# Moving the second copies of the mLSTM query tiles by DMA inside SBUF

## The chip, the cores and the metric

One core of a Trainium2 chip runs the whole program; inputs and outputs lie in HBM. The metric is device time in microseconds (us) of one execution, taken as the median over several runs. The engines are TensorE (PE; its weight loads are shown as PEld), VectorE (DVE), ScalarE (ACT), GpSimd (POOL) and SyncE (SP); each works through its own queue of instructions in order and waits on semaphores for the others.

## The reference

A two-layer model on 512 tokens of width 1024 in float32. Layer one is a dilated window attention, layer two an mLSTM; each is followed by a SwiGLU feed-forward block of inner width 2816, and a final RMS norm ends it. The part that matters here is the mLSTM mixer, cut to its core:

```python
qk = silu(causal_depthwise_conv(xn @ w_qk, conv_w, conv_b))
q  = heads(qk[..., :512], 64)                 # 8 heads of 64
k  = heads(qk[..., 512:], 64) * 64 ** -0.5
...
w_intra = exp(dmat - m_t[..., None])          # decay from the gates
sm  = w_intra * einsum('bhtd,bhsd->bhts', q, k)
num = einsum('bhts,bhsv->bhtv', sm, v) + ...  # state carried from earlier chunks
den = sum(sm, axis=-1) + ...
h   = num / maximum(abs(den), exp(-m_t))[..., None]
h   = h * rsqrt(mean(h * h, axis=-1, keepdims=True) + eps)
out = (h * head_gain * sigmoid(o_pre)) @ w_out
```

The kernel does not carry a state from chunk to chunk: it forms the 512 x 512 scores of each head below the diagonal and weighs them with the decay.

## The kernel before

**Tiling.** Activations lie transposed, features on the 128 partitions and the 512 tokens along the free dimension. Each float32 operand of a large matmul is split into a high part in the format float32r and the rest in the same format, and a product is the sum of three matmuls (`SPLITS`): high by high, low by high, high by low. Weights come from HBM in chunks of 512 KB on SP's queue, ACT makes the high part (line 208) and DVE the low part (line 209), three chunks deep.

**The mLSTM stage.** `project_qk` and `convolve` make the query tiles `qk[0..3]` and the key tiles `qk[4..7]` (128 partitions hold two heads of 64): DVE multiplies by the norm's factor (line 1139) and adds four shifted products (lines 1146 and 1148), ACT applies SiLU (line 1150). `project_v` makes the values; ACT writes them to `vaug` (line 1161). The order of projections is: pairs of query and key tiles, then values, then the output gates (`mo`), then `mwo`, the output projection.

**The stacks.** `stack(p)` prepares the operands of the score matmuls of heads 2p and 2p+1. A head has only 64 features, so 128 partitions hold two things at once: `ks` has the high part of the keys on the head's own half of the partitions and the low part on the other half. `qs` has the high part of the queries on both halves, and `ql` the low part on both halves. One matmul of `ks` with `qs` then gives high by high plus low by high, and one with `ql` adds the rest. Own and other half are the slices `own` and `oth`. Before the change ACT writes both halves of `qs` (lines 1291 and 1292); DVE writes the own half of `ql` (line 1294), and POOL copies it to the other half (line 1295). Each of `ks`, `qs`, `ql` has two buffers per position in the pair, so that the third call of `stack` reuses the tiles of the first.

**Per head.** `decay` makes a matmul into the single PSUM buffer with tag `t` (name m0nb for head 0), DVE adds the causal mask to it (m0d, line 1306) and ACT takes exponentials from both (m0e, lines 1311 and 1314). `scores` multiplies (PE, lines 1324 and 1325, into two buffers with tag `s`) and DVE weighs (line 1326). `numerators` multiplies by the values (line 1336), ACT sums squares (line 1350), DVE takes three Newton steps for the root (lines 188 to 193) and scales (m0yt, line 1357). `outputs` transposes on PE (m0yT, line 305, again the buffer `t`), and ACT copies (line 1366).

**Order.** Work that lies beside the projections is put off to counted ticks, one for each weight chunk; `STACK_AT` and `HEAD_AT` give the ticks:

```python
STACK_AT = (9, 11, 15, 17)
HEAD_AT = ((9, 10, 12, 14), (10, 11, 13, 15), (12, 13, 15, 17), ...
```

Within these limits the framework's scheduler, at build time, fixes the order of the instructions of each engine from estimated durations, and places the semaphores. An edit to one instruction can therefore change the order of others.

Of the kernel before, what the change touches and what calls it, by code (L numbers as in the profile page):

```python
# [11 lines left out]
F32 = mybir.dt.float32  # L12
F32R = mybir.dt.float32r
I32 = mybir.dt.int32
AF = mybir.ActivationFunctionType
# [55 lines left out]
def tile_hybrid_dilated_attn_mlstm(  # L71
# [4 lines left out]
    nc = tc.nc  # L76
# [3 lines left out]
    def pool(stack, name, **kw):  # L80
        return stack.enter_context(tc.tile_pool(name=name, bufs=1, **kw))
# [1039 lines left out]
    with ExitStack() as mctx:  # L1121
# [160 lines left out]
        def stack(p):  # L1282

            for i in range(2):
                own, oth = slice(i * 64, i * 64 + 64), slice(64 - i * 64, 128 - i * 64)
                q, k = qk[p][own], qk[4 + p][own]
                ks = mp.tile([P, SEQ], F32R, tag="ks%d" % i, name="ks%d_%d" % (p, i), bufs=2)
                qs = mp.tile([P, SEQ], F32R, tag="qs%d" % i, name="qs%d_%d" % (p, i), bufs=2)
                nc.scalar.activation(ks[own], k, AF.Copy)  # L1289
                nc.vector.tensor_tensor(ks[oth], k, ks[own].bitcast(F32), op=ALU.subtract)  # L1290
                nc.scalar.activation(qs[own], q, AF.Copy)
                nc.scalar.activation(qs[oth], q, AF.Copy)  # L1292
                ql = mp.tile([P, SEQ], F32R, tag="ql%d" % i, name="ql%d_%d" % (p, i), bufs=2)
                nc.vector.tensor_tensor(ql[own], q, qs[own].bitcast(F32), op=ALU.subtract)
                nc.gpsimd.tensor_copy(ql[oth], ql[own].bitcast(F32))
                stacks[2 * p + i] = (ks, qs, ql)

        y = [None] * H
# [72 lines left out]
        for p, t in enumerate(STACK_AT):  # L1371
            at_tick(t, lambda p=p: stack(p))
# [161 lines left out]
```

## Time and profile before

| | us |
|---|---|
| median of 3 runs | 1432.88 (1432.66 to 1432.92) |
| the profiled execution | 1432.49 |
| its span, first to last instruction | 1430.7 |
| PE busy | 1418.7 (99%) |
| DVE busy | 955.7 (67%) |
| ACT busy | 604.6 (42%) |
| POOL busy | 61.1 (4%) |

The span is what the profile shows; the profiled execution took 1.8 us more than its span. Durations in the text are of that one execution. In the timelines the first number is the start in us from the span's beginning, the second the time in us that a row takes together; idle time ahead of a row and what ended it stand in brackets. Matmuls are pipelined, so that the rows of PE overlap and the distance between two starts is what one costs. In part 5 of a page and in the waits a wait for several semaphores is put down to the one that came last by the profile.

### The profile page before, as it was taken

How to read it: one execution, taken by the hardware profiler on the slowest of the kernel's cores; microseconds unless marked ns; L12 is line 12 of the kernel's file. 1: busy time of each engine (PE TensorE's matmuls, PEld its weight loads, DVE VectorE, ACT ScalarE, POOL GpSimd, SP SyncE). 2: the span in 40 equal slices, each digit the busy share in tenths (PEclk: the TensorE clock that was granted, in tenths of full speed). 3: DMA queues.
4: the chain of work that ended last, by engine and by line, in shares of the span. 5: the costliest groups of instructions: out<-in, count | busy, mean ns of one | idle time of the engine just before them, and what ended most of it. 6: DMA issues, size and time to landing. Idle time of an engine off the chain costs nothing. (4 is left out here: it accounts for less than half of the span.)

```text
span 1430.7 us, 20253 instructions
## 1 busy us (share of the span) xinstructions
PE 1418.7 (99%) x8018; PEld 1244.3 (87%) x8018; DVE 955.7 (67%) x1671; ACT 604.6 (42%) x1025; POOL 61.1 (4%) x101
## 2 busy tenths in 40 slices
PE   9999999999999999999999999999999999999997
PEld 7888888888888888999998888888888899998886
DVE  7857556556567397787782358897758777888233
ACT  5333224224215253444462233696534354455123
POOL 1001001001001000000000010110000000001001
PEclk9999999999999999999999999999999999999999
DMA  6326225234334434323232332312133332236331
GB/s 198 97 89 198 75 89 181 92 98 128 136 101 109 145 111 133 99 79 118 89 97 96 96 98 75 104 59 61 51 115 95 123 118 85 93 118 182 113 112 65
DMA packets 132088, 154.46 MB, mean 108 GB/s; under 512 B 6485, under 2 KB 120469, under 8 KB 131993
## 3 DMA queue, kind: packets, MB, share of 16 engines
q1 hardware_dynamic: 125616, 131.55, 29.4%
q0 software_dynamic: 4720, 20.49, 4.8%
q8 instruction: 63, 1.03, 0.3%
q10 hardware_dynamic: 1656, 1.12, 0.2%
q14 instruction: 33, 0.26, 0.1%
HBM read 141.09 MB, written 12.06 MB: 107 GB/s over the span
## 5 line engine op out<-in xcount | busy, mean ns | idle before, releaser
L1463 PE MATMUL fin<-fw_l,f1hh 128*128 128x512 f32 (+1 forms) x198 | 72.5, 366 | 0.0
L1463 PE MATMUL fin<-fw_h,f1hh 128*128 128x512 f32 (+1 forms) x198 | 72.4, 366 | 0.0
L1463 PE MATMUL fin<-fw_h,f1hl 128*128 128x512 f32 (+1 forms) x198 | 72.4, 365 | 0.0
L209 DVE TENSOR_TENSOR fo_k_l<-fo_k_w,fo_k_h 128x1024 fp32r<-128x1024 f32 (+1 forms) x24 | 27.2, 1134 | 62.0 <-ACT fo_k_h L208 62.0
L239 PE MATMUL fo<-f0hh,fo_k_h 128*128 128x512 f32 x176 | 68.5, 389 | 0.0
L239 PE MATMUL fo<-f0hl,fo_k_h 128*128 128x512 f32 x176 | 68.5, 389 | 0.0
L239 PE MATMUL fo<-f0hh,fo_k_l 128*128 128x512 f32 x176 | 68.5, 389 | 0.0
L209 DVE TENSOR_TENSOR fw_l<-fw_w,fw_h 128x1024 fp32r<-128x1024 f32 x22 | 27.0, 1232 | 59.9 <-ACT fw_h L208 59.9
L208 ACT ACTIVATE fo_k_h<-fo_k_w 128x1024 fp32r<-128x1024 f32 (+1 forms) x24 | 23.7, 989 | 74.7 <-PE fo L239 74.7
L208 ACT ACTIVATE fw_h<-fw_w 128x1024 fp32r<-128x1024 f32 x22 | 23.3, 1060 | 67.5 <-PE fin L1463 67.0
L1463 PEld LDWEIGHTS fin<-fw_l,f1hh 128*128 128x128 f32 x198 | 37.4, 189 | 6.2 <-DVE fw_l L209 0.2
L1463 PEld LDWEIGHTS fin<-fw_h,f1hh 128*128 128x128 f32 x198 | 37.4, 189 | 6.1
L1463 PEld LDWEIGHTS fin<-fw_h,f1hl 128*128 128x128 f32 x198 | 37.3, 188 | 6.0
L239 PEld LDWEIGHTS fo<-f0hh,fo_k_l 128*128 128x128 f32 x176 | 33.0, 188 | 6.9
L239 PEld LDWEIGHTS fo<-f0hl,fo_k_h 128*128 128x128 f32 x176 | 33.0, 188 | 6.9
L239 PEld LDWEIGHTS fo<-f0hh,fo_k_h 128*128 128x128 f32 x176 | 33.0, 188 | 6.7
L239 PE MATMUL f0j<-n_h,f0j_h 128*128 128x512 f32 x96 | 37.5, 390 | 0.0
L239 PE MATMUL f1j<-n_h,f1j_h 128*128 128x512 f32 x96 | 37.5, 390 | 0.0
L239 PE MATMUL f1j<-n_h,f1j_l 128*128 128x512 f32 x96 | 37.4, 389 | 0.0
L239 PE MATMUL f0j<-n_h,f0j_l 128*128 128x512 f32 x96 | 37.4, 389 | 0.0
L239 PE MATMUL f0j<-n_l,f0j_h 128*128 128x512 f32 x96 | 37.3, 389 | 0.0
L239 PE MATMUL f1j<-n_l,f1j_h 128*128 128x512 f32 x96 | 37.3, 389 | 0.0
(2101 smaller groups left out, 4863.2 us busy)
## 6 DMA issues: line engine op xcount, KB each, us to landing
f0j_w<-in_ffn_w_in_dram SPq DMA_DIRECT2D x28, 512.0 KB, 4.4
f1j_w<-in_ffn_w_in_dram SPq DMA_DIRECT2D x28, 512.0 KB, 3.6
fw_w<-in_ffn_w_out_dram SPq DMA_DIRECT2D x22, 512.0 KB, 3.9
fo_k_w<-in_ffn_w_out_dram SPq DMA_DIRECT2D x20, 512.0 KB, 3.5
awo_k_w<-in_attn_w_out_dram SPq DMA_DIRECT2D x8, 512.0 KB, 6.8
mv_k_w<-in_mlstm_w_in_dram SPq DMA_DIRECT2D x8, 512.0 KB, 3.7
mqk_k_w<-in_mlstm_w_in_dram SPq DMA_DIRECT2D x8, 512.0 KB, 3.8
mo_k_w<-in_mlstm_w_in_dram SPq DMA_DIRECT2D x8, 512.0 KB, 3.7
```

Of the source, the lines that this page charges most:

```text
L208: nc.scalar.activation(hi[:, :n], raw[:, :n], AF.Copy)
L209: nc.vector.tensor_tensor(lo[:, :n], raw[:, :n], hi[:, :n].bitcast(F32), op=ALU.subtract)
L239: nc.tensor.matmul(acc, whl[a][:, k, m * P:(m + 1) * P], pairs[b][kk], start=(kk == 0 and (a, b) == SPLITS[0]), stop=(kk == nk - 1 and (a, ...
L1463: nc.tensor.matmul(acc[i][:, cs], a[a_][kk][:, tb * P:(tb + 1) * P], whl[b_][:, k, cs], start=(kk == 0 and (a_, b_) == SPLITS[0]), stop=(k ...
```

## The change

In `stack`, for each of the eight heads, two copies to the other half of the partitions change their maker. The other half of `qs` was written by ACT from the float32 tile `q`; it is now a DMA from the own half of `qs`. The other half of `ql` was copied by POOL; it is now a DMA from the own half of `ql`. Both DMAs are issued from POOL's queue.

```diff
@@ -1289,10 +1289,10 @@
                 nc.scalar.activation(ks[own], k, AF.Copy)
                 nc.vector.tensor_tensor(ks[oth], k, ks[own].bitcast(F32), op=ALU.subtract)
                 nc.scalar.activation(qs[own], q, AF.Copy)
-                nc.scalar.activation(qs[oth], q, AF.Copy)
+                nc.gpsimd.dma_start(qs[oth], qs[own])
                 ql = mp.tile([P, SEQ], F32R, tag="ql%d" % i, name="ql%d_%d" % (p, i), bufs=2)
                 nc.vector.tensor_tensor(ql[own], q, qs[own].bitcast(F32), op=ALU.subtract)
-                nc.gpsimd.tensor_copy(ql[oth], ql[own].bitcast(F32))
+                nc.gpsimd.dma_start(ql[oth], ql[own])
                 stacks[2 * p + i] = (ks, qs, ql)
```

The instructions of SP stand in the same order before and after. On PE, DVE and ACT the first place where the order differs is in the mLSTM stage, and the number of matmuls, of DVE instructions and of ACT table loads is the same; ACT has eight instructions fewer, POOL eight casts fewer and sixteen DMA issues more.

## The prediction

> **What bounds the kernel now.** I read the page first, then the table of windows, TensorE's waits, and the timelines of PE, DVE and ACT around the edited lines.
>
> ```profile
> span 1430.7 us, 20253 instructions
> ...
> PE 1418.7 (99%) x8018; PEld 1244.3 (87%) x8018; DVE 955.7 (67%) x1671; ACT 604.6 (42%) x1025; POOL 61.1 (4%) x101
> ```
>
> TensorE is busy for 1418.7 of 1430.7 us. An engine beside it costs time only where PE waits for it. The edited copies run between 898 and 962 us; the table of windows gives span, then busy time and instructions of PE, PEld, DVE, ACT and POOL:
>
> ```profile
> 895.00:915.00 20.00, 20.00 (x142) 18.29 (x141) 19.70 (x30) 14.69 (x21) 2.80 (x3) 1.00 0.36 106
> 915.00:935.00 20.00, 19.62 (x104) 16.44 (x103) 15.98 (x29) 13.96 (x31) 1.67 (x1) 1.00 0.29 83
> 935.00:955.00 20.00, 20.00 (x126) 17.68 (x125) 19.32 (x56) 19.80 (x51) 2.20 (x2) 1.00 0.16 49
> 955.00:975.00 20.00, 18.33 (x124) 16.74 (x123) 15.39 (x47) 14.69 (x34) 1.75 (x2) 1.00 0.21 58
> ```
>
> PE is full, but here its two helpers nearly are too: DVE has 19.70 of 20 us in the first window, ACT 19.80 in the third. PE's waits from 880 to 1060 us:
>
> ```profile
> PE m1yT L305 <- ACT vaug L1161: 1.7, 1, 1.7
> PE m1nb L1304 <- ACT m0e L1314: 0.4, 1, 0.4
> ```
>
> So 2.1 us is all that a lighter ACT or DVE can give back in this stage, and a later instruction on DVE or ACT is paid in full if PE waits for it at these two places, or at a new one.
>
> **The change part by part.** *Removed.* The tile views of qs and ql give the old copies:
>
> ```profile
> L1292 ACT ACTIVATE qs<-mqk x8: 627/630/630, 899.0 to 958.4; 64x512 fp32r<-64x512 f32 x8
> ```
> ```profile
> L1295 POOL CAST ql<-ql x8: 612/1100/1667, 901.5 to 960.5; 64x512 fp32r<-64x512 f32 x8
> ```
>
> ACT loses 8 x 0.63 = 5.0 us, POOL 8 casts of 0.6 to 1.7 us. Neither bounds the kernel, so by themselves they are worth 0, or up to 2.1 us if they end PE's two waits (a rival below).
>
> *Added.* Sixteen copies of 64 x 512 x 4 bytes = 128 KB go onto POOL's queue. Nearest rows (issues with KB and median us to landing, then POOL's timeline):
>
> ```profile
> hD<-hB POOLq DMA_DIRECT2D x8, 256.0 KB, 5.8
> ...
> a3pT<-a3pD POOLq DMA_DIRECT2D x2, 960.0 KB, 9.3
> ...
> out_dram<-fo SPq DMA_DIRECT2D x4, 256.0 KB, 2.1
> ```
> ```profile
> 121.01 2.22 POOL L684 DMA_DIRECT2D a0pD<-a0pB  x4 [107.12 <-DVE a0pB L681]
> ...
> 1276.16 2.63 POOL L1422 DMA_DIRECT2D hD<-hB  x4 [238.09 <-DVE hB L1419]
> ```
>
> No transfer inside SBUF is in this trace, and none with fp32r tiles at both ends. I bound the landing by 2.1 and 9.3 us and take 5, near the 5.8 us of the POOL queue's own 256 KB transfers. An issue takes 2.22/4 = 0.56 us; POOL has the room. What hides the landing is the distance from ql's subtraction on DVE to the first score matmul that reads it. It is shortest for the first pair of heads: ql is complete at 900.67 + 1.40 = 902.07, and PE reads it at 915.94.
>
> ```profile
> 900.67 1.40 DVE L1294 TENSOR_TENSOR ql<-mqk,qs 64x512 fp32r<-64x512 f32 x2
> ```
> ```profile
> 915.94 0.40 PE L1325 MATMUL m0s<-ql,ks 128*128 128x512 f32 x1
> ```
> ```profile
> L1324 PE MATMUL m2s<-qs,ks x4: 220/346/390, 938.2 to 940.5; 128*128 128x512 f32 x1, 128*128 128x384 f32 x1, 128*128 128x256 f32 x1, 128*128 128x128 f32 x1
> ...
> L1324 PE MATMUL m6s<-qs,ks x4: 284/350/393, 991.2 to 994.4; 128*128 128x512 f32 x1, 128*128 128x384 f32 x1, 128*128 128x256 f32 x1, 128*128 128x128 f32 x1
> ```
>
> That is 13.9 us of cover; even 9.3 us plus three queued issues (1.7) is inside it. For later pairs the cover is longer (the last old cast starts at 960.5, its pair's first score at 991.2), and POOL's in-order queue (the third pair's second qs stands behind its first ql, which waits for DVE) has the same cover. Behind the sixteen copies POOL has nothing but a memset until the residual transfers at 1276 us. ACT's write of the third pair's qs reuses the first pair's buffer and must now also wait for that copy, due by 902.07 + 9.3 = 911 us; the buffer is read until the scores from 915.94 on anyway. SP's order of weight loads is unchanged. So the transfers cost 0; each microsecond of landing over 13.9 would cost one.
>
> *Moved.* The instruction order is fixed when the program is built, and the new order differs on PE, DVE and ACT. Three moves matter.
>
> (A) On DVE the second pair's two subtractions (L1294) go ahead of the convolution of the key tiles, instead of after the mask addition of head 0 (m0d); on ACT the last ks copy (L1289) goes ahead of head 0's exponentials, instead of after them. The rows of before, DVE, ACT and PE:
>
> ```profile
> 896.37 0.48 DVE L1146 TENSOR_SCALAR conv<-pre,cols 128x512 f32<-128x512 f32 x1
> ...
> 902.83 0.67 DVE L1146 TENSOR_SCALAR conv<-pre,cols 128x512 f32<-128x512 f32 x1
> ...
> 913.11 0.67 DVE L1294 TENSOR_TENSOR ql<-mqk,qs 64x512 fp32r<-64x512 f32 x1
> ...
> 914.52 1.00 DVE L1294 TENSOR_TENSOR ql<-mqk,qs 64x512 fp32r<-64x512 f32 x1
> ```
> ```profile
> 911.79 0.72 ACT L1150 ACTIVATE mqk<-conv,cols 128x512 f32<-128x512 f32 x1 [0.79 <-DVE conv L1148]
> ...
> 913.19 1.28 ACT L1311 ACT_TABLE_LOAD   x1
> ...
> 916.63 0.38 ACT L1314 ACTIVATE m0e<-m0nb,bcol 128x128 f32<-128x128 f32 x1
> ...
> 918.78 0.63 ACT L1289 ACTIVATE ks<-mqk 64x512 fp32r<-64x512 f32 x1
> ```
> ```profile
> 917.07 0.50 PE L1304 MATMUL m1nb<-mneg,sel 128*128 128x512 f32 x1 [0.38 <-ACT m0e L1314]
> ```
>
> Two subtractions back to back take 1.40; the convolution step that ran beside a POOL cast took 0.67 where its clean form takes 0.48, so 0.19 goes with the cast: the key tile's convolution ends 1.40 - 0.19 = 1.2 us later. ACT was waiting for exactly that (0.79 of idle time, ended by conv), so its SiLU, table load and exponentials move by 1.2, and by 0.63 more for the ks copy put in front. The last read of head 0's PSUM tile (916.63) and with it the next matmul into that single buffer, m1nb, come 1.2 + 0.63 = 1.8 us later; with the semaphores of the new neighbours I take 1.9. PE already waited there, so all of it is lost: **+1.9** (1.2 if the ks copy found idle time, 2.1 at most).
>
> (B) At m1yT PE waits 1.67 us:
>
> ```profile
> 941.55 0.15 DVE L1354 TENSOR_TENSOR m0rr<-m0rr,m0rq_y 128x4 f32<-128x4 f32 x1
> ...
> 942.79 0.68 DVE L1139 TENSOR_TENSOR pre<-mqk,n2rbc 128x512 f32<-128x512 f32 x1
> ...
> 958.50 0.69 DVE L1290 TENSOR_TENSOR ks<-mqk,ks 64x512 fp32r<-64x512 f32 x1
> 959.22 0.46 DVE L1354 TENSOR_TENSOR m1rr<-m1rr,m1rq_y 128x4 f32<-128x4 f32 x1
> ...
> 960.43 1.13 DVE L1357 TENSOR_SCALAR m1yt<-m1num,m1rr 128x128 f32<-128x128 f32 x4
> 961.47 1.22 DVE L209 TENSOR_TENSOR mo_k_l<-mo_k_w,mo_k_h 128x1024 fp32r<-128x1024 f32 x1
> ```
> ```profile
> 958.86 0.28 PE L271 MATMUL mv<-mv_k_h,n_h 128*128 128x256 f32 x1
> 958.98 0.28 PE L271 MATMUL mv<-mv_k_l,n_h 128*128 128x256 f32 x1
> 960.93 0.30 PE L305 MATMUL m1yT<-cst,m1yt 128*128 128x128 f32 x1 [1.67 <-ACT vaug L1161]
> ```
>
> The list names vaug, but m1yT reads m1yt, whose first piece starts at 960.43. In the new DVE order the 1.22 us split of mo_k_l moves ahead of m1yt, a ks subtraction of 0.69 moves behind it, and the stretch that casts put on rows like 959.22 (0.46 where its kind takes 0.15) goes; together about 0. So m1yt is late by what PE is late. But the new PE order puts five more value matmuls (0.12 us from start to start) ahead of m1yT: 0.6 of the wait is filled. Against that I keep 0.1 for DVE: **-0.5** (bounds -1.7, the whole wait, and 0).
>
> (C) Later, the second halves of the scores of heads 5, 6 and 7 and the transposes m3yT and m6yT change places with projection matmuls, and on DVE their predecessors stand between Newton steps and gate multiplications (128x512, as L1139 above 0.68 us). None of these places waits in before. Each of five (m3yT, m6s, m7s, m6yT, first use of yo_l) may get a wait between 0 and 0.7; I take 0.3, near the one short wait of the list (0.4): **+1.5** (0 to 3.5).
>
> Sum 1.9 - 0.5 + 1.5 = **+2.9 us**. The profiled execution took 1432.49 us, its span 1430.7 plus 1.8 around it; the median of the runs is 1432.88. On the median: **1435.8 us**. This case's own range adds the ends: 1.2 - 1.7 + 0 = -0.5, and 2.1 + 0 + 3.5 = +5.6, so 1432.4 to 1438.5.
>
> **The rivals.** *Not slower: ACT's returned time decides.* If it is really vaug on ACT that ends m1yT's wait, as the list says, four qs copies (2.5 us) leave ACT ahead of it after 933 us, the 1.67 us go, and with no loss at m1nb the 0.38 too: 1432.88 - 2.1 = 1430.8. It decides if ACT and not the DVE convolution is last ahead of m0e. Against it stands the 0.79 us idle ended by conv. Chance 0.07.
>
> *Absorbed.* If DVE has room so that m1yt does not move with PE, the 1.67 us wait swallows most of the 1.9, and (C) is zero: +0.2, 1433.1. For it: DVE loses the cast stretches. Against: it is 19.32 of 20 us busy there. Chance 0.15.
>
> *The transfers arrive late.* If the landing in this stage is over 13.9 us, PE stands at m0s: at 18 us it is +4.1 on top of +2.9, 1439.9. Chance 0.10, because issues in the trace beside DVE's work keep 0.56 us, and the longest landing is 9.3. [...] The trace shows the contention for casts (0.67 against 0.48 above) and not for the issue rows.
>
> **How the numbers follow.** Forecast case 0.68, rivals 0.07, 0.15, 0.10. A measurement of this kernel can tell about 0.2%, 2.9 us, from no change. The forecast sits on that bound. Its lower end needs m1yT's whole wait to go, which DVE at 19.32 of 20 us makes unlikely, while new waits at more places than five only add; so of its 0.68 I put 0.44 above the bound and 0.24 within. With the late transfers slower has 0.54; same is 0.24 + 0.15 = 0.39; faster 0.07. The range from 1432.4 to 1438.5 leaves out the gain, most of the late transfers and little else.
>
> **What would show it.** Right: PE's waits name m1nb with about 2.3 us, m1yT with about 1.1, and some of 0.2 to 0.6 at m3yT, m6s, m7s, m6yT; DVE shows L1294 four times before 907 us; the DMA part shows the copies landing in 2 to 9 us; conv rows beside them stay at 0.48. Wrong: m1nb's wait stays at 0.4, or PE waits at L1324 or L1325 for a DMA.

## The result and the profile after

The changed kernel takes 1437.18 us (median, 1436.16 to 1437.64), the kernel before 1432.93 (1432.44 to 1433.49): slower by 4.25 us, ratio 1.0029, 95% interval 1.0018 to 1.0039. The profiled execution took 1436.49 us, 4.0 more than that of before. First the busy times on the page, then the windows of the prediction:

```profile
span 1434.7 us, 20276 instructions
...
PE 1420.0 (99%) x8018; PEld 1245.1 (87%) x8018; DVE 954.8 (67%) x1671; ACT 599.2 (42%) x1017; POOL 60.7 (4%) x109
```
```profile
895.00:915.00 20.00, 20.00 (x137) 18.14 (x136) 19.68 (x31) 10.53 (x15) 4.10 (x8) 1.00 0.66 159
915.00:935.00 20.00, 17.84 (x99) 15.12 (x98) 13.93 (x24) 13.20 (x31) 0.00 (x0) 1.00 0.27 80
935.00:955.00 20.00, 20.00 (x119) 17.50 (x118) 19.15 (x58) 19.36 (x49) 2.55 (x5) 1.00 0.34 86
955.00:975.00 20.00, 18.89 (x132) 17.50 (x131) 15.15 (x46) 14.70 (x35) 1.53 (x3) 1.00 0.30 73
```

ACT has its 4 us back in the first window (10.53 for 14.69). PE has lost 1.8 us in the second (17.84 for 19.62) and found 0.6 in the fourth (18.89 for 18.33). TensorE's waits between 880 and 1060 us name the places, and the timelines of PE and DVE show them:

```profile
PE m1nb L1304 <- ACT m0e L1314: 2.2, 1, 2.2
PE m1yT L305 <- DVE m1yt L1357: 1.1, 1, 1.1
PE m6yT L305 <- DVE m6yt L1357: 0.3, 1, 0.3
```
```profile
919.85 0.50 PE L1304 MATMUL m1nb<-mneg,sel 128*128 128x512 f32 x1 [2.16 <-ACT m0e L1314]
...
963.39 0.30 PE L305 MATMUL m1yT<-cst,m1yt 128*128 128x128 f32 x1 [1.11 <-DVE m1yt L1357]
```
```profile
901.68 1.40 DVE L1294 TENSOR_TENSOR ql<-mqk,qs 64x512 fp32r<-64x512 f32 x2
...
904.85 0.67 DVE L1294 TENSOR_TENSOR ql<-mqk,qs 64x512 fp32r<-64x512 f32 x1
905.45 0.47 DVE L1146 TENSOR_SCALAR conv<-pre,cols 128x512 f32<-128x512 f32 x1
905.95 0.69 DVE L1294 TENSOR_TENSOR ql<-mqk,qs 64x512 fp32r<-64x512 f32 x1
```

The transfers themselves are fast: DMA issues with KB and median us to landing, and the tile view of qs with the issue's own ns:

```profile
qs<-qs POOLq DMA_DIRECT2D x8, 128.0 KB, 4.0
...
ql<-ql POOLq DMA_DIRECT2D x8, 128.0 KB, 2.9
```
```profile
L1292 POOL DMA_DIRECT2D qs<-qs x8: 509/512/529, 900.2 to 958.1; - x8
```

But the stage explains only a part of the 4.0. I followed the start of one and the same instruction through both traces. The first pair of rows is a0g0q on PE, before and after; the second the last group of PE in the chain that ended last; the third is POOL's drains, from the view of the program's last line (shortest/median/longest ns of three; the longest is the one that counts, below "the long drain"):

```profile
8.34 0.50 PE L449 MATMUL a0g0q<-xa_h,first_h 128*128 128x512 f32 x1 [0.51 <-ACT first_h L439]
```
```profile
9.25 0.49 PE L449 MATMUL a0g0q<-xa_h,first_h 128*128 128x512 f32 x1 [0.51 <-ACT first_h L439]
```
```profile
1302.54 120.80 PE fin L1463 x594
```
```profile
1305.25 120.80 PE fin L1463 x594
```
```profile
L1530 POOLq DRAIN  x3: 46/98/5512, 1424.4 to 1430.4; - x3
```
```profile
L1530 POOLq DRAIN  x3: 46/98/6817, 1427.1 to 1434.4; - x3
```

So PE is 0.9 late at the first product, 1.0 late in front of the edited stage, 2.7 late behind it: the stage costs 1.7. At the end POOL's long drain, which nothing in the edit names, takes 6.82 us instead of 5.51, and in both profiles the program ends 0.8 us after it: 1.3 more. The 1.0 at the start has to be scatter or a cost; in ten further profiles below, with and without transfers, the same lag against the one profile of before lies anywhere between -0.1 and 1.1 us, so it is scatter of the start. It goes with the granted clock, whose first record of 1.00 begins at 4.69 us in the trace of before and at 7.22 us in that of the changed kernel: the first matmuls of the program (line 107, 128x512) start 0.43 us apart ahead of it and 0.23 behind it. Over all twelve profiles this record begins between 4.39 and 7.69 us, and a later one always goes with a later a0g0q (8.03 to 9.35 us).

That gave three theories to test. **Order**: the stage loses because the scheduler moved the second pair's subtractions and the ks copy (term A). **Drain**: POOL's long drain takes 0.082 us more for each DMA issued from POOL's queue in the whole program (57 before, 73 after). **Transfers**: each copy by DMA costs something where it runs. A fourth, the **clock**, came from the first round.

### The profile page after: what moved, and what is told of

Same layout as the page of the kernel before. It is cut to its first block, busy times and chain, and to the rows that moved or that the text cites. A ratio compares the mean times of both kernels' runs of the same rounds, so it can differ in the third digit from the quotient of the medians.

```text
span 1434.7 us, 20276 instructions
## 1 busy us (share of the span) xinstructions
PE 1420.0 (99%) x8018; PEld 1245.1 (87%) x8018; DVE 954.8 (67%) x1671; ACT 599.2 (42%) x1017; POOL 60.7 (4%) x109
```

## The experiments

All ran with timed rounds beside the kernel before. "Lag" is how much later the same matmul of the last feed-forward stage starts than in the profile of before, less the same difference ahead of the edited stage. The diffs are cut to the lines that matter, with long lines broken.

| kernel | POOL's DMAs | m1nb's wait | lag over the stage | long drain | median less before's |
|---|---|---|---|---|---|
| before | 57 | 0.4 | 0 | 5.51 | 0 |
| changed | 73 | 2.2 | +1.7 | 6.82 | +4.25 |
| changed, second round (after_again) | 73 | 2.2 | +1.6 | 6.81 | +3.9 |
| qs_alone | 65 | 3.3 | +5.5 | 6.16 | +7.2 |
| ql_alone | 65 | 0.3 | -0.6 | 6.16 | +0.4 |
| sub_late | 73 | 0.6 | +0.1 | 6.82 | +1.2 |
| on_sp | 57 | 2.2 | +3.2 | 5.51 | +2.9 |
| order_alone | 57 | 1.4 | +1.7 | 5.51 | +1.8 |
| small64 | 121 | 0.4 | 0.0 | 10.74 | +5.2 |
| filled9 | 73 | none | +1.6 | 6.82 | +2.9 |
| ks_late | 73 | 1.5 | +1.0 | 6.82 | +2.35 |
| best | 47 | none | -1.0 | 4.69 | -1.9 |

**One kind of copy at a time.** qs_alone is the kernel before with only the line of qs changed, ql_alone with only that of ql.

```diff
-                nc.scalar.activation(qs[oth], q, AF.Copy)
+                nc.gpsimd.dma_start(qs[oth], qs[own])      # qs_alone
...
-                nc.gpsimd.tensor_copy(ql[oth], ql[own].bitcast(F32))
+                nc.gpsimd.dma_start(ql[oth], ql[own])      # ql_alone
```

> Only the second copies of qs go by DMA (8 transfers); those of ql stay casts on POOL. The instructions of PE, DVE and ACT stand in the order of the changed kernel. Three theories for the 4.25 us between the medians. Order theory: the stage loses because the second pair's subtractions stand ahead of the key convolution, so m1nb waits again about 2.5 us (2.2 in the changed kernel, a little more because the casts beside the convolution are back), and PE's lag over the stage is about +1.9. Drain theory: POOL's last instruction, its drain, takes 0.083 us for each DMA that POOL has issued (4.75 us after the last operation for 57 in the kernel before, 6.06 for 73 in the changed one), so the end is later by 8 x 0.083 = 0.66. Together about +2.5, 1435.4 us, plus up to 1 us by which the start scatters. Transfer theory (each copied tile costs something): half of the change's 4.25, 1435.0, with m1nb's wait at half, about 1.3.

> Only the second copies of ql go by DMA (8 transfers); ACT writes both halves of qs as before. PE, DVE and ACT have exactly the order of the kernel before. Order theory: the stage loses nothing, m1nb waits 0.4 or less (0.2 if the cast's stretch of 0.19 on the convolution goes), m1yT 1.7; drain theory: the end is 0.66 later; together +0.5 to +0.7, 1433.5 us. Transfer theory: half of 4.25, 1435.0, with new waits of PE at the scores.

Measured 1440.05 us (ratio 1.0051, interval 1.0037 to 1.0065) and 1433.22 (1.0002, 0.9993 to 1.0011). The eight transfers of ql are as good as free, those of qs alone cost more than both together: the transfer theory, which wanted 1435.0 twice, falls. What tells them apart is that taking the copy from ACT changes the scheduler's order and taking the cast from POOL does not. qs_alone came out 4.6 us above my number. One part is that the casts that stayed now run beside the subtractions and the convolution that were moved ahead; its DVE timeline has rows that the changed kernel has at 0.69 and 0.75:

```profile
905.63 0.98 DVE L1294 TENSOR_TENSOR ql<-mqk,qs 64x512 fp32r<-64x512 f32 x1
906.64 1.19 DVE L1148 SCALAR_TENSOR_TENSOR conv<-pre,cols,conv 128x512 f32<-128x512 f32 x1
```

so that m1nb waits 3.3 us instead of 2.5. The other part is in its table of windows (span, busy and count of PE, PEld, DVE, ACT, POOL, then the granted clock):

```profile
915.00:920.00 5.00, 1.99 (x14) 1.57 (x13) 4.21 (x7) 4.91 (x13) 0.00 (x0) 1.00 0.39 117
920.00:925.00 5.00, 4.75 (x16) 4.01 (x17) 2.78 (x5) 5.00 (x16) 0.00 (x0) 0.66 0.01 2
```

After the long wait the granted clock is 0.66 over 5 us. That is the clock theory: 0.34 x 5 = 1.7 us of PE's time are lost to it. Some 1.1 us of this kernel's median (7.2 less the stage's 5.5 and the drain's 0.65) stay unexplained; m1yT waits 1.9 us in it, and a second such window in other executions would fit, but its profile shows none.

**The order taken back, the transfers kept.** In sub_late the second pair's subtractions may not pass m0d.

```diff
-                nc.vector.tensor_tensor(ql[own], q, qs[own].bitcast(F32), op=ALU.subtract)
+                with tc.issue_after(masked[0]) if p == 1 else nullcontext():   # masked[0]: m0d of head 0
+                    nc.vector.tensor_tensor(ql[own], q, qs[own].bitcast(F32), op=ALU.subtract)
```

> All sixteen transfers as in the change, but the second pair's two subtractions on DVE are held behind the mask addition of head 0, where the kernel before has them. Order theory: m1nb's wait falls from 2.2 to 0.4 to 0.6, m1yT keeps 1.1, and the stage comes out between -0.4 and +0.2 against the kernel before; the drain's +1.3 stays: 1.8 us under the changed kernel, about 1434.2 to 1435.4. Transfer theory: m1nb's wait stays, 1437.2.

Measured 1434.00 (1.0010, 1.0001 to 1.0018). All sixteen transfers run, the wait falls to 0.6 us and the stage's loss is gone (+0.1). The scheduler then also put both ks copies of the second pair behind m0e, so this edit takes back more than its one line. What is left, 1.2 us, is the drain's 1.3.

**The queue changed, the order kept.** on_sp issues the sixteen transfers from SP.

```diff
-                nc.gpsimd.dma_start(qs[oth], qs[own])
+                nc.sync.dma_start(qs[oth].bitcast(F32), qs[own].bitcast(F32))
...
-                nc.gpsimd.dma_start(ql[oth], ql[own])
+                nc.sync.dma_start(ql[oth].bitcast(F32), ql[own].bitcast(F32))
```

> The changed kernel with its sixteen transfers issued from SP's queue instead of POOL's; PE, DVE and ACT keep the changed kernel's order. Order theory: the stage's loss stays, m1nb 2.2 and m1yT 1.1, PE's lag over the stage +1.7. Drain theory: POOL's last drain is back at 5.5 us and the end comes 1.3 sooner than in the changed kernel, about 1435.9. If weight loads behind the transfers on SP come late, PE waits at a weight product; I expect none, as the chunks are loaded three ahead. Transfer theory: 1437.2, as the copies are the same.

Measured 1435.70 (1.0019, 1.0011 to 1.0028). The drain is back at 5.51, no weight product waits, and the three waits are those of the changed kernel to 0.1 us. Yet the lag is 3.2, not 1.7. The windows show where, and PE's row why:

```profile
918.79 0.50 PE L1304 MATMUL m1nb<-mneg,sel 128*128 128x512 f32 x1 [2.15 <-ACT m0e L1314]
```
```profile
915.00:920.00 5.00, 2.85 (x16) 2.24 (x16) 3.69 (x6) 4.99 (x15) 0.00 (x0) 0.94 0.38 105
920.00:925.00 5.00, 5.00 (x19) 4.16 (x19) 1.93 (x4) 4.13 (x13) 0.00 (x0) 0.72 0.21 46
```

After an idle time of 2.15 us the granted clock lost (0.06 + 0.28) x 5 = 1.7 us; the trace has it at 0.5 for 3.41 us, and the lag is 1.5 more than the changed kernel's. In the changed kernel's profile the same wait of 2.16 us was followed by a clock of 1.00:

```profile
915.00:920.00 5.00, 2.84 (x21) 2.42 (x20) 4.07 (x6) 4.95 (x14) 0.00 (x0) 1.00 0.36 107
920.00:925.00 5.00, 5.00 (x24) 4.17 (x25) 2.62 (x4) 5.00 (x16) 0.00 (x0) 1.00 0.06 4
```

So the drop depends on more than the wait's length, and the clock records of the traces show on what. In both traces with a drop (qs_alone and on_sp) the clock stands at 1.00 for 914.77 us ahead of it and for 508.59 us behind it, and in those of before and of the changed kernel for 1423.36 us without a break; these are 268, 149 and 417 times 3.4133, so in these traces the clock changed at the edges of windows of that length. Counted on from the first rise of the clock, on_sp's wait (916.63 to 918.79) lies whole in one window (916.02 to 919.44), and the drop begins at its end. In the changed kernel an edge at 918.58 cuts the wait into 0.90 and 1.26 us, in its second profile (after_again) one at 918.14 into 0.69 and 1.46. Over all windows counted so in the twelve traces, each with 2.15 us or more without PE work is followed by a clock of 0.5, and each with up to 1.91 us by 1.00 (qs_alone's wait of 1.9 us at m1yT among them); no window lies between.

**The order alone, without a transfer.** order_alone is the kernel before with one number changed.

```diff
-STACK_AT = (9, 11, 15, 17)
+STACK_AT = (9, 9, 15, 17)
```

> No transfer at all: the kernel before, with the second call of stack given out at tick 9 instead of 11. Both moves of term A come with it (the second pair's two subtractions on DVE ahead of most of the key convolution, the last ks copy on ACT ahead of head 0's exponentials), PE's order stays that of the kernel before. Order theory: m1nb waits 1.3 to 2.4 us instead of 0.4, m1yT keeps about 1.7, the lag over the stage is +1.0 to +2.0, the drain at the end keeps 5.5 us; about 1434.4 us. Should m1nb's wait be near 2 or more, some executions lose another 1.7 to a window of half clock. Transfer theory: without a transfer nothing is lost, 1432.9.

Measured 1434.91 (1.0013, 1.0004 to 1.0022). No transfer is added and 1.8 us are lost, as much as the lag of its stage. A wait of 1.4 us at m1nb (0.4 before) and a new one of 0.5 at a value product make up 1.5 of it:

```profile
PE m1yT L305 <- ACT vaug L1161: 1.7, 1, 1.7
PE m1nb L1304 <- ACT m0e L1314: 1.4, 1, 1.4
PE mv L271 <- DVE mv_k_l L209: 0.5, 1, 0.5
```

**The drain alone.** small64 adds 64 transfers of 4 bytes to the kernel before, where nothing waits.

```diff
+        spare = fp.tile([P, 64], F32, name="spare")
+        [nc.gpsimd.dma_start(spare[:1, i:i + 1], cols[:1, i:i + 1]) for i in range(64)]
```

> The kernel before with 64 tiny transfers of 4 bytes added on POOL's queue in the last feed-forward stage, into a tile that nobody reads. Nothing waits for them and the instruction order of PE, DVE and ACT is unchanged. If POOL's last drain takes 0.082 us for each DMA issued from its queue, it grows by 64 x 0.082 = 5.25 to about 10.8 us, and the kernel takes 1438.1. If it goes by bytes or by descriptors, of which these have few, it grows by well under 2 us, to under 1435. If the drain has nothing to do with DMAs, 1432.9.

```profile
L1530 POOLq DRAIN  x3: 46/98/10737, 1425.4 to 1436.7; - x3
```

Measured 1438.32 (1.0037, 1.0024 to 1.0049): +5.23, where 64 x 0.082 = 5.25. The price is per DMA, not per byte: (10.737 - 5.512) / 64 and (6.817 - 5.512) / 16 are both 0.082.

**The wait filled.** filled9 is the changed kernel with nine matmuls that nobody reads ahead of m1nb (m1nb is issued right behind them, and the third and fourth score pairs of head 0 then stand ahead of two projection matmuls, not between them).

```diff
+            fill = ps.tile([P, 512], F32, tag="o", name="fill", bufs=2)
+            for i in range(9):
+                with tc.issue_after(last_on_pe()):
+                    nc.tensor.matmul(fill, sel[:, 1, :], mneg, start=True, stop=True)
```

> The changed kernel with nine matmuls (128x512, about 0.22 us each) whose result nobody reads, put into PE's wait ahead of m1nb. Clock theory: the wait of 2.2 us lets the granted clock drop to 0.5 for one window of 3.4 us in most executions, which costs 1.7 us there; the profiled execution of the changed kernel was one without it. With PE kept busy no execution drops, m1nb starts when it did, and the median falls by 1.0 to 1.7, to 1435.5 to 1436.2, with the runs closer together. If the drop has another cause, or costs nothing, 1437.2 as before; if the fill delays m1nb, above that.

```profile
917.32 2.22 PE L1321 MATMUL fill<-mneg,sel 128*128 128x512 f32 x9
919.64 0.50 PE L1324 MATMUL m1nb<-mneg,sel 128*128 128x512 f32 x1
```

Measured 1436.01 (1.0020, 1.0011 to 1.0029). m1nb starts when it did (919.64 with PE 0.8 late at the start; 919.85 with 1.0), and the median falls by 1.2 us (0.9 against the changed kernel's second round) although PE does more. The runs lie between 1435.3 and 1436.3, those of the changed kernel between 1436.2 and 1437.6.

**The ACT half of term A alone.** ks_late holds the last ks copy behind head 0's exponentials.

```diff
-                nc.scalar.activation(ks[own], k, AF.Copy)
+                with tc.issue_after(weighed[3]) if (p, i) == (1, 1) else nullcontext():  # weighed[3]: last copy of m0e
+                    nc.scalar.activation(ks[own], k, AF.Copy)
```

> The changed kernel with only the ACT half of term A taken back: the last ks copy is held behind head 0's exponentials, the second pair's subtractions stay ahead of the key convolution. Order theory: m1nb's wait falls by one copy, 0.63, from 2.2 to 1.5 or 1.6; m1yT 1.1; the drain's +1.3 stays. Clock theory: with a wait of 1.5, as in the run without transfers that had 1.4, no execution loses a half-clock window, so the median falls by 0.63 and by the 1.2 that the windows cost on average, to 1435.3; if waits of 1.5 still bring it, 1436.5.

Measured 1435.42 (1.0016, 1.0007 to 1.0025). The wait falls from 2.16 to 1.50, by one copy, and the median by 1.5 against the same round's run of the changed kernel (1.8 against the first): the copy's 0.66 and about 1 us more. Its profile shows a clock of 1.00 behind the wait of 1.5 us.

**The changed kernel again.**

> The changed kernel once more, unchanged, for a second profiled execution and in the same round as the run before. The profiled execution shown so far had no half-clock window behind m1nb although it waited 2.16 us there; clock theory: most executions have one, so this profile shows the granted clock at 0.5 for 3.4 us after the wait with about 3 in 4, and PE's lag over the stage is then 1.7 + 1.7 = 3.4 instead of 1.7. The median is 1437 again. If no execution has one, the remaining 1.2 us of the medians are unexplained.

Measured 1436.95 (1.0028, 1.0016 to 1.0039). The profiled execution again had a clock of 1.00 behind the wait; it is also the shortest of the seven (1436.12), the others reach 1437.57. So the drop is seen in the profiles of qs_alone and on_sp, and no profile of the changed kernel itself shows it. Its other executions do speak of it. One window of 3.41 us at 0.5 takes 0.0012 off the mean granted clock of an execution; this mean is 0.996 or 0.997 in seven of the changed kernel's fifteen timed executions, all of 1436.88 us or more, and 0.998 or 0.999 in all 33 of sub_late, filled9 and ks_late, which end in the same drain. How often the drop comes, and so its 1.2 us on the median, is known only from these means and medians.

**A version from what was found.** best keeps ACT's two copies of qs, and with them the old order on PE, moves ql's second copy to SP's queue, gives the second stack call tick 10, and issues the last residual's ten transfers from SP.

```diff
-STACK_AT = (9, 11, 15, 17)
+STACK_AT = (9, 10, 15, 17)
...
-                nc.gpsimd.tensor_copy(ql[oth], ql[own].bitcast(F32))
+                nc.sync.dma_start(ql[oth].bitcast(F32), ql[own].bitcast(F32))
...
-                nc.gpsimd.dma_start(d.rearrange("(b i) a x -> a i b x", i=R)[a_],
+                nc.sync.dma_start(d.rearrange("(b i) a x -> a i b x", i=R)[a_],
...
-                nc.gpsimd.dma_start(t, d.rearrange("(c p) a x -> p c (a x)", p=P))
+                nc.sync.dma_start(t, d.rearrange("(c p) a x -> p c (a x)", p=P))
```

> What the theories would choose: qs written twice by ACT as in the kernel before (its order kept), the second copy of ql by DMA from SP's queue, the second call of stack at tick 10 instead of 11 so that the last ks copy leaves ACT's path to m0e, and the ten transfers of the last residual (hD, ht) issued from SP instead of POOL. Order theory: m1nb's wait under 0.2, m1yT 1.4, lag over the stage -0.6 to -1.0. Drain theory: 47 DMAs left on POOL, the drain 0.82 shorter, of which 0.65 counts until SP's own last step ends later. Together -1.2 to -1.6: 1431.3 to 1431.7. If weight loads behind the transfers on SP come late, PE waits at a weight product and the gain is gone.

```profile
PE m1yT L305 <- DVE m1yt L1357: 1.4, 1, 1.4
```
```profile
L1530 POOLq DRAIN  x3: 46/98/4693, 1423.6 to 1428.8; - x3
```
```profile
L1530 SPq DRAIN  x3: 7/7/7, 1428.2 to 1428.5; - x3
```

Measured 1431.23 against 1433.09 (0.9988, 0.9979 to 0.9996): faster than both, by a little more than expected. m1nb waits no more, and POOL's long drain (1423.6 + 4.7 = 1428.3) ends with SP's last steps (1428.2), so that still fewer DMAs on POOL should bring little; no run tried it.

## Why the prediction came out right, step by step

The forecast of 1435.8 lies 1.4 below the measured 1437.2 and inside its range, but its sum was put together differently from the 4.25 that was measured. The forecast's +2.9 was the stage alone. The parts measured are +1.7 for the stage, +1.3 for the drain, and about +1.2 for the clock (the median's fall in filled9; 0.9 against the second round).

- **(A) m1nb, forecast +1.9.** Right: 0.38 became 2.16, +1.8. L1294 stands four times before 907 us, the convolution row beside it is 0.47. ks_late splits it: one copy, 0.66 (forecast 0.63), the rest 1.1 (forecast 1.2). order_alone shows that the order does it without any transfer.
- **(B) m1yT, forecast -0.5.** Right: 1.67 became 1.11. In before, ql_alone and the changed kernel m1yT starts 0.50, 0.49 and 0.50 us behind the start of m1yt's row on DVE, but 0.89, 0.53 and 2.37 us behind that of vaug's row on ACT: m1yt, not vaug, ended the wait. In the trace four more value matmuls stand ahead of m1yT (five were counted), which is 0.48 of the 0.56.
- **(C) five small waits, forecast +1.5.** This is the mis-sized term. Of the five places only m6yT waits, 0.3 us. The whole stage lost 1.7, so what is left beside A and B is 1.7 - 1.8 + 0.6 = 0.5. sub_late has the changed kernel's order on PE, with all these changes of place, and its stage lost 0.1. A change of place in PE's order at a spot where neither neighbour waits is worth far less than the 0.3 each that I took from the one short wait in the list.
- **"So the transfers cost 0."** Right for the stage: landing 4.0 and 2.9 us (taken 5), issue 0.51 (taken 0.56), cover 13.9, no wait at L1324 or L1325; sub_late runs all sixteen with a lag of 0.1. Wrong for the program: I followed POOL's queue only to the residual transfers and not to its last instruction, where each DMA costs 0.082 us. That is +1.3.
- **The clock** was not in the sum. I took a wait's price to be its length.
- **The rivals.** ACT's returned time bought nothing: qs_alone returned all of it and is the slowest kernel here, and sub_late, which returned it with the order ahead of m1nb taken back, has a lag of +0.1. The loss was not absorbed: m1yT's wait took up 0.6 of A's 1.8, and C was not zero. The transfers were not late, although DVE was busy for 19.7 of 20 us in the first window: an issue took 0.51 us there too.

That the range held is in part luck: the overestimate in C (1.0 us) and the two missing terms (2.5 us) partly cancelled.

## What to carry to other kernels

Where a scheduler orders the engines, compare the order after the edit before costing the edit: here the removed ACT copy cost nothing and saved nothing, and the reordering it caused cost 1.7 us. Read the chain to the very last instruction, since a queue can be charged at the end for what it did all along (here 0.082 us for each DMA on POOL's queue); plain copies belong on a queue without such a charge (here SP's, with which the long drain was back at 5.51 us). A wait of PE of about 2 us may cost its length and a stretch of half clock behind it (3.41 us at 0.5 behind the 2.15 us of on_sp, none behind the 2.16 us of the changed kernel's profile), depending on where the windows of the clock fall in that execution, so shorten the longest wait first, or fill it.

## What the runs showed of the hardware

- POOL's long drain at the end takes 0.082 us more for each DMA issued from POOL's queue, of 4 bytes or of 128 KB alike (4.69, 5.51, 6.16, 6.82 and 10.74 us for 47, 57, 65, 73 and 121). The same transfers from SP's queue add nothing to it (5.51 us in on_sp, as in before).
- In the traces the granted clock changed at the edges of windows of 3.41 us counted from its first rise (it stood at 1.00 for 914.77, 508.59 and 1423.36 us, each a multiple), and the first rise came at 4.69 us in the profile of before and at 7.22 in the changed kernel's. A window with 2.15 us or more without PE work was followed by a clock of 0.5, one with up to 1.91 us by 1.00. So one and the same wait of 2.15 us brought the clock down in one profile (on_sp) and not in two others (the changed kernel's). The drop in on_sp was 1.7 us of clock and made the lag 1.5 us longer.
- A copy of 64 x 512 float32 from one half of the partitions to the other lands in 2.9 (ql) and 4.0 us (qs; both medians of eight) from POOL's queue, while DVE was busy for 13.93 to 19.68 of each 20 us. With casts of the same size on POOL beside them (qs_alone), two rows of DVE took 0.98 and 1.19 us that the changed kernel has at 0.69 and 0.75.
